# Gate and up products of eight feed-forward networks: one 512-column product for the high weights

## Chip, cores and metric

The kernel runs on one core of a Trainium2 chip. The metric is the device time of one execution in microseconds. Before the change the median of three runs is 2490.16 us (2488.91 to 2493.22).

## What is computed

Two transformer-like blocks of depth 2 work on 256 tokens of 1024 features in float32. Each layer of each block holds two feed-forward networks around a mixer, eight networks in all. What matters here is the network itself, in the first and in the second block:

```python
def swiglu(x, w_gate, w_up, w_down):
    return (jax.nn.silu(x @ w_gate) * (x @ w_up)) @ w_down
...
h = h + 0.5 * swiglu(rmsnorm(h, ffn1_norm[l]), ffn1_w_gate[l], ffn1_w_up[l], ffn1_w_down[l])
...
x = x + 0.5 * rms_norm(swiglu_2(rms_norm(x, ln_ffn1_pre[l]), w_ffn1_in[l], w_ffn1_out[l]),
                       ln_ffn1_post[l])
```

The weights are 1024 x 2816 (gate, up) and 2816 x 1024 (down). `swiglu_2` is the same with gate and up in one matrix. The second block's networks have a norm after them (the post norm) with an eps of its own.

## The kernel before

Activations lie feature-major: tiles of 128 features by 256 tokens. TensorE multiplies in the type float32r. So that float32 precision is kept, every operand is split into a high part (a copy rounded to float32r, on ScalarE, line 408) and a low part (the difference, on VectorE, line 409), in `split`. A product is the sum of three: high·high, high weights·low activations, low weights·high activations. `mm3` (line 325) issues these three for one k-tile of 128 features and 128 output columns, the weights stationary, 256 token columns moving.

`weights` (line 291) loads a weight chunk of 128 x 2048 in two halves of 512 KB (tag `raw`, four buffers, all on SP's queue in program order) and splits it in four parts of 512 columns (tags `wh` and `wl`, eight buffers each, hence two chunks). A part of a gate or up chunk holds two k-tiles of 256 output columns.

`gemm` (line 339) multiplies one chunk, or several together, over eight k-tiles: the k-tile is the outer loop, the two halves of 128 output columns the inner one. Both halves lie in one PSUM bank of 512 columns, 256 each. `ffn` (line 628) walks over 11 groups of 256 hidden features (`NG`). The first step runs gate 0, up 0 and gate 1 together; after that each step has a gate chunk, an up chunk and the down product of the step before. The gate result is multiplied by the token factor of the norm (line 662) and goes through silu (line 663), the up result is multiplied in (line 666), and the outcome is split into `hh` and `hl` for the down product, which sums in four banks (`acc`) over all steps. The last down product takes its weights from buffers of its own (`dh`, `dl`) and is issued in a chained order, each output tile being evacuated as it is done.

PSUM has eight banks: `mm` two, `st` one (norm sums), and in a feed-forward network `acc` four and `up` one. Gate uses `mm`, up uses `up` (in step 1 one of `acc`). `Act` holds the split activations as two separate sets of tiles (high, low), four feature tiles to an allocation.

`Norm.finish` (line 481) and `rstd` (line 370) give the token factor of a norm; it is applied after the product. `Post.finish` (line 584) computes the post norm of a second-block network: line 595 scales the sum of squares and adds eps, line 596 takes the power on GpSimd. The order of the instructions on each engine is found by the framework's scheduler, which simulates the program; only what is chained (`chain`) or loaded (`fetch`) keeps its written order.

Of the kernel before, what the change touches and what calls it, by code (L numbers as in the profile page):

```python
# [18 lines left out]
P = 128  # L19
# [192 lines left out]
# ---------------------------------------------------------------- device  # L212
# [8 lines left out]
def bc(x, n):  # L221
    """[128, m] repeated n times along a new middle dimension."""
    return x.unsqueeze(1).to_broadcast([x.shape[0], n, x.shape[1]])


class Net:
    def __init__(s, tc, ctx, A):
# [4 lines left out]
            dict(x=1, vec=1, cst=1, msk=1, mhalf=1, zero=1, cs=2, raw=4, wh=8, wl=8, act=8, sq=3, rb=3,  # L232
# [19 lines left out]
    # ---- allocation: a tag's tiles come in program order, each tag has its own buffers  # L252
# [58 lines left out]
    def chain(s, ins):  # L311
        """Issue behind the last chained instruction of its engine."""
# [12 lines left out]
    def mm3(s, out, w, c, n, a, start, stop, pin=lambda i: i):  # L325
        """Feature-major product of a k-tile: weight columns c..c+n stationary, a = (hi, lo) [128, 256]."""
        w = w.cols(c, n)
        for i, (x, y) in enumerate(((0, 0), (0, 1), (1, 0))):
            pin(s.nc.tensor.matmul(out, lhsT=w[x], rhs=a[y], start=start and i == 0,  # L329
                                   stop=stop and i == 2, skip_group_check=True))  # L330

    def mm3t(s, out, w, c, n, a, h, start, stop):
        """Token-major product of a k-tile, token half h: activations stationary."""
        w = w.cols(c, n)
        for i, (x, y) in enumerate(((0, 0), (1, 0), (0, 1))):
            s.nc.tensor.matmul(out, lhsT=a[y][:, h * P:h * P + P], rhs=w[x], start=start and i == 0,
                               stop=stop and i == 2, skip_group_check=True)
# [22 lines left out]
    def gemm_t(s, ap, act, tag="mm"):  # L360
        """Token-major: 256 output columns, both token halves in one bank."""
# [15 lines left out]
    def colsum(s, sq):  # L377
        """Sum over partitions of [128, 256] -> PSUM [128 tokens, 2]."""
# [6 lines left out]
    def spread_ps(s, r, pin=lambda i: i):  # L385
        """Per-token [128, 2] -> PSUM [128, 256] on every partition."""
# [6 lines left out]
    def warm(s, tag, n):  # L393
        """Products of zeros while TensorE waits: its clock halves after 3.4 us of rest."""
# [9 lines left out]
    def split(s, hi, lo, src, gain=None, pin=lambda i: i):  # L404
        """hi + lo = src * gain, each exact in float32r."""
# [9 lines left out]
class Weight:  # L415
    """A split weight chunk in parts of m columns."""
# [10 lines left out]
class Wide:  # L427
    """n feature tiles of [128, 256], four to an allocation, allocated at their first use."""
# [16 lines left out]
class Act:  # L445
    """Feature tiles split for the tensor engine."""

    def __init__(a, s, n, tag="act"):
        a.hi, a.lo = Wide(s, n, tag, F32R), Wide(s, n, tag, F32R)

    def __getitem__(a, k):
        return a.hi[k], a.lo[k]


class Norm:
    """RMS norm ahead of a GEMM: x * gain split as it is made, the token factor kept apart."""
# [6 lines left out]
    def tile(n, k, pin=lambda i: i):  # L463
        if n.gain:
            n.s.split(*n.act[k], n.s.x[:, k], n.s.v(n.gain, k), pin)
# [22 lines left out]
class Final(Norm):  # L488
    """The first block's final norm and the second's first: both token factors are left for after the GEMM."""
# [7 lines left out]
    def tile(n, k, pin=lambda i: i):  # L497
        n.s.split(*n.act[k], n.s.x[:, k], n.both[:, k:k + 1], pin)
# [11 lines left out]
    def finish(n):  # L510
# [8 lines left out]
        r2, _ = s.rstd(w, 2, D)  # L519
        nc.vector.tensor_tensor(n.r, n.r1, r2, op=ALU.mult)  # L520

# [7 lines left out]
class Post:  # L529
    """RMS norm of a GEMM's result (four banks of two tiles), added to the residual. The tiles come in ORDER:  # L530
    the last one alone is left when the rest have been summed."""
# [22 lines left out]
    def step(p, o, bank, late=False):  # L554
        """Tile o is in its bank [128, 2, 256]; `late` leaves the gain to scale()."""
# [14 lines left out]
        # all but the last three tiles in one  # L570
# [13 lines left out]
    def finish(p, eps, half, nxt, out=None):  # L584
        """eps: a number; half: a power of two"""
# [9 lines left out]
        s.chain(nc.vector.tensor_scalar(v, p.sum[:, 0:2], 1.0 / (D * half * half), eps / (half * half), op0=ALU.mult, op1=ALU.add))  # L595
# [32 lines left out]
def ffn(s, nrm, wg, wu, wd, evac, ws=None, ahead=None, pre=None, mid=None):  # L628
# [5 lines left out]
    def down(j, h, last):  # L634
# [6 lines left out]
        for kk, o in order:  # L641
            s.mm3(acc[o // 2][:, (o % 2) * T:(o % 2 + 1) * T], w, kk * D + o * P, P,
                  (h[0][:, kk], h[1][:, kk]), j == 0 and kk == 0 and o % 2 == 0, last and kk == 1,
# [4 lines left out]
    g2 = None  # L648
    for j in range(NG):
        if j == 0:  # L650
            g, u, g2 = s.gemm([wg[j], wu[j], wg[1]], act, ("mm", "up", "mm"), ws=ws)
# [26 lines left out]
FFN_SB = dict(ga=3, hh=3, hl=3, dh=4, dl=4)  # L678
# [3 lines left out]
def ffn_a(s, nrm, l, f, nxt, ws=None, ahead=None, pre=None, mid=None):  # L682
    """h += 0.5 * swiglu(rmsnorm(h))"""
# [77 lines left out]
def softmax_rows(s, sc):  # L761
    """sc [128, 2, nk] in SBUF -> exp(sc - max) in place, and 1/sum [128, 2]."""
# [9 lines left out]
def transposed(s, blocks):  # L772
    """Up to four [128, 128] blocks -> their transposes side by side in SBUF."""
# [18 lines left out]
def mix_a(s, nrm, l, nxt, ws, ahead):  # L792
    with s.phase("ma", dict(th=6, y=4, qk=4, cc=4, sc=3, pT=2, qm=2, lam=3, o8=2, **SMX),
# [4 lines left out]
def _mix_a(s, nrm, l, nxt, ws, ahead):  # L798
# [4 lines left out]
    # latents, pool input  # L803
# [8 lines left out]
    cqa = (s.t2("pT", F32R), s.t2("pT", F32R))  # L812
    for k in range(2):
        s.split(cqa[0][:, k], cqa[1][:, k], cq[:, k], s.v(f"a_qn_{l}", k))
    cka = (s.tile([P, T], "row", F32R), s.tile([P, T], "row", F32R))
    s.split(cka[0], cka[1], ckv, s.v(f"a_kvn_{l}"))
# [15 lines left out]
    # MLA up projections  # L832
# [3 lines left out]
    for c in range(3):  # L836
        b = s.ps("S")
        for k in range(2):
            for j in range(2):
                o = (2 * c + j) * P  # L840
                s.mm3(b[:, j * T:(j + 1) * T], wq, k * 768 + o, P, (cqa[0][:, k], cqa[1][:, k]), k == 0 and j == 0, k == 1)
# [39 lines left out]
    ym, yd, yp = Act(s, 4, "y"), Act(s, 4, "qk"), Act(s, 4, "y")  # L881
# [4 lines left out]
    pq = Act(s, 4, "th")  # L886
# [835 lines left out]
```

## Time and profile before

| | |
|---|---|
| median of three runs | 2490.16 us |
| lowest, highest run | 2488.91, 2493.22 us |
| profiled execution: span from first to last instruction | 2484.6 us |
| TensorE products | 19980 |
| TensorE, VectorE, ScalarE busy | 98%, 69%, 56% |
| mean granted clock of TensorE | 0.994 |

The profile is of one execution. Its page gives the span; what lies around the span in that execution is in no view, and the median of the runs is 5.56 us above it. PE is TensorE, PEld its weight loads, DVE VectorE, ACT ScalarE, POOL GpSimd and SP the queue that issues the loads. L329 is line 329 of the kernel; products of many places carry this line, so they are told apart by their tiles: `mm<-act,wh` writes a bank of the tag mm from activations and high weights. A matmul record lasts longer than the distance to the next one, because products are pipelined: the pace is read from starts or from a run of many.

### The profile page before, as it was taken

To read this page: it belongs to the slowest core of one execution; us is meant where nothing else is said; L and a number is where in the kernel's file an instruction comes from. 1 tells how busy PE (TensorE), PEld (TensorE's weight loads), DVE (VectorE), ACT (ScalarE), POOL (GpSimd) and SP (SyncE) were. 2 spreads that over 40 slices of the span, in tenths; PEclk is the share of its full clock that TensorE was granted. 3 is DMA by queue.
4 is the path that set the end of the run, shared out by engine and by line. 5 is a ranking of instruction groups with operands and counts; after the bars stand their busy time and mean duration, and the time that the engine had idled before them with its cause. 6 is when DMAs were issued, how large, how long until landed. Compare 5 with 4: busy or idle time off the path is not lost. (4 is left out here: it accounts for less than half of the span.)

```text
span 2484.6 us, 50434 instructions
## 1 busy us (share of the span) xinstructions
PE 2434.8 (98%) x19980; PEld 2390.1 (96%) x19980; DVE 1724.5 (69%) x3259; ACT 1381.2 (56%) x2598; POOL 42.9 (2%) x43
## 2 busy tenths in 40 slices
PE   8999999999999999999999999999999999999998
PEld 8999999999999989999999988999989998899997
DVE  6557888656756888865675588776666568877665
ACT  5556665555555676555555564465565556346554
POOL 0000000000000000000000000000000000000000
PEclk9999999999999999999999999999999999999999
DMA  6554444555555444555555532156535553215651
GB/s 228 184 186 156 144 140 170 192 185 191 173 184 184 142 147 145 170 195 182 176 182 183 189 129 85 37 171 205 187 111 179 186 197 120 85 43 170 205 191 59
DMA packets 110525, 396.91 MB, mean 160 GB/s; under 512 B 12752, under 2 KB 13264, under 8 KB 110288
## 3 DMA queue, kind: packets, MB, share of 16 engines
q1 hardware_dynamic: 109008, 391.33, 48.2%
q8 instruction: 156, 2.56, 0.4%
q10 hardware_dynamic: 1280, 2.36, 0.3%
q14 instruction: 81, 0.66, 0.1%
HBM read 392.60 MB, written 1.05 MB: 158 GB/s over the span
## 5 line engine op out<-in xcount | busy, mean ns | idle before, releaser
L409 DVE TENSOR_TENSOR wl<-raw,wh 128x512 fp32r<-128x512 f32 (+1 forms) x1446 | 984.0, 688 | 583.3 <-ACT wh L408 571.1
L408 ACT ACTIVATE wh<-raw 128x512 fp32r<-128x512 f32 (+1 forms) x1446 | 897.7, 628 | 842.8 <-PE mm L329 310.2
L329 PE MATMUL mm<-act,wh 128*128 128x256 f32 x4992 | 941.1, 286 | 18.6 <-ACT wh L408 9.0
L329 PEld LDWEIGHTS mm<-act,wh 128*128 128x128 f32 x4992 | 784.2, 191 | 27.9 <-ACT wh L408 9.3
L329 PE MATMUL mm<-act,wl 128*128 128x256 f32 x2496 | 709.3, 285 | 0.0
L329 PEld LDWEIGHTS mm<-act,wl 128*128 128x128 f32 x2496 | 476.8, 191 | 2.6 <-issue 1.7
L329 PE MATMUL up<-act,wh 128*128 128x256 f32 x2560 | 469.9, 284 | 0.8 <-ACT wh L408 0.8
L329 PEld LDWEIGHTS up<-act,wh 128*128 128x128 f32 x2560 | 401.6, 193 | 1.1 <-ACT wh L408 1.1
L329 PE MATMUL up<-act,wl 128*128 128x256 f32 x1280 | 363.2, 284 | 0.0
L329 PE MATMUL acc<-hl,wh 128*128 128x256 f32 x1280 | 358.6, 281 | 0.0
L329 PE MATMUL acc<-hh,wl 128*128 128x256 f32 x1280 | 358.6, 281 | 0.0
L329 PE MATMUL acc<-hh,wh 128*128 128x256 f32 x1280 | 357.5, 281 | 0.0
L329 PEld LDWEIGHTS up<-act,wl 128*128 128x128 f32 x1280 | 246.3, 192 | 0.0
L329 PEld LDWEIGHTS acc<-hh,wl 128*128 128x128 f32 x1280 | 243.1, 190 | 0.0
L329 PEld LDWEIGHTS acc<-hl,wh 128*128 128x128 f32 x1280 | 242.8, 190 | 0.0
L329 PEld LDWEIGHTS acc<-hh,wh 128*128 128x128 f32 x1280 | 242.0, 190 | 0.0
L666 DVE TENSOR_TENSOR ga<-up,ga 128x512 f32<-128x512 f32 x80 | 55.3, 691 | 18.3 <-PE up L329 13.3
L408 ACT ACTIVATE hh<-ga 128x512 fp32r<-128x512 f32 x88 | 55.5, 631 | 19.9 <-DVE ga L666 19.7
L662 DVE TENSOR_TENSOR ga<-mm,rb 128x512 f32<-128x512 f32 x88 | 60.0, 689 | 9.3 <-PE mm L329 9.3
L409 DVE TENSOR_TENSOR hl<-ga,hh 128x512 fp32r<-128x512 f32 x88 | 60.8, 691 | 6.1
L411 ACT ACTIVATE act<-x,vec 128x256 fp32r<-128x256 f32 x104 | 47.6, 500 | 28.1 <-DVE x L606 21.7
L663 ACT ACTIVATE ga<-ga 128x512 f32<-128x512 f32 x88 | 54.7, 629 | 14.6 <-DVE ga L662 14.5
(498 smaller groups left out, 2811.9 us busy)
## 6 DMA issues: line engine op xcount, KB each, us to landing
raw<-a_wgate SPq DMA_DIRECT2D x88, 512.0 KB, 3.7
raw<-a_wup SPq DMA_DIRECT2D x88, 512.0 KB, 3.8
raw<-a_wdown SPq DMA_DIRECT2D x88, 512.0 KB, 3.7
raw<-b_wgate SPq DMA_DIRECT2D x88, 512.0 KB, 4.0
raw<-b_wup SPq DMA_DIRECT2D x88, 512.0 KB, 4.1
raw<-b_wdown SPq DMA_DIRECT2D x88, 512.0 KB, 4.1
raw<-a_win SPq DMA_DIRECT2D x80, 512.0 KB, 3.7
raw<-a_wbr SPq DMA_DIRECT2D x24, 512.0 KB, 3.8
```

The costliest lines, as they stand in the source:

```text
L329: pin(s.nc.tensor.matmul(out, lhsT=w[x], rhs=a[y], start=start and i == 0, stop=stop and i == 2, skip_group_check=True))
L408: pin(nc.scalar.activation(hi, src, AF.Copy))
L409: pin(nc.vector.tensor_tensor(lo, src, hi.bitcast(F32), op=ALU.subtract))
L411: pin(nc.scalar.activation(hi, src, AF.Copy if isinstance(gain, float) else AF.Identity, scale=gain))
L662: nc.vector.tensor_tensor(ga, two(g), bc(rb, 2), op=ALU.mult)
L663: nc.scalar.activation(ga, ga, AF.Silu)
L666: nc.vector.tensor_tensor(ga, two(u), ga, op=ALU.mult)
```

## The change

For gate and up a new `mm2` takes the place of `mm3`: the high weights are loaded once and meet high and low activations in one product of 512 columns, which fills a bank (high·high in the first 256 columns, high·low in the second); the low weights meet the high activations in 256 columns, added to the first half. Each half of 128 output columns now has a bank of its own. A new `join` adds the two halves of each bank: ScalarE copies the second half to SBUF, VectorE adds the first. The loop over the halves is outermost for a chunk alone and innermost for the three chunks together. The banks of the later chunks are dealt in turn from `mm`, `mm`, `up`; the first three chunks use `mm` and all of `acc`.

So that high and low lie side by side, `Act` holds them in one tile; the mixers' uses of `Act` follow, with some temporary tiles under other tags, and the differential attention's result is split in two parts instead of one. The split of the network's hidden features goes into one tile `h`. The product with the token factor and the product with the gate read joined tiles in SBUF.

In second-block networks the eps of the post norm is multiplied by the token variance of the norm before it (`er`, one operation of 128x2 for a network), and line 595's operation takes `er` as an operand; `Final` multiplies its two variances.

```diff
+    def mm2(s, bank, w, c, a, start, stop):
+        hi, lo = w.cols(c, P)
+        s.nc.tensor.matmul(bank, lhsT=hi, rhs=a.rearrange("p a t -> p (a t)"), start=start, stop=False, skip_group_check=True)
+        s.nc.tensor.matmul(bank[:, :T], lhsT=lo, rhs=a[:, 0], start=False, stop=stop, skip_group_check=True)
+
+    def join(s, out, banks):
+        for i, b in enumerate(banks):
+            t = s.tile([P, T], "jn")
+            s.nc.scalar.activation(t, b[:, T:], AF.Copy)
+            s.nc.vector.tensor_tensor(out[:, i], b[:, :T], t, op=ALU.add)
+
+    def gemm2(s, aps, act, tags, ws=None):
+        ws = ws or s.weights(aps)
+        bs = [[s.ps(t) for t in tags[2 * i:2 * i + 2]] for i in range(len(ws))]
+        def tile(k, w, b):
+            for j in range(2):
+                s.mm2(b[j], w, k * T + j * P, act[k], k == 0, k == 7)
+        if len(ws) > 1:
+            for k in range(6):
+                for w, b in zip(ws, bs):
+                    tile(k, w, b)
+            for w, b in zip(ws, bs):
+                tile(6, w, b)
+                tile(7, w, b)
+        else:
+            for j in range(2):
+                for k in range(8):
+                    s.mm2(bs[0][j], ws[0], k * T + j * P, act[k], k == 0, k == 7)
+        return bs
...
+    order = ("mm", "mm", "up")
+    turn = [0]
+    def tags():
+        t = [order[(turn[0] + i) % 3] for i in range(2)]
+        turn[0] += 2
+        return t
...
-            g, u, g2 = s.gemm([wg[j], wu[j], wg[1]], act, ("mm", "up", "mm"), ws=ws)
+            g, u, g2 = s.gemm2([wg[j], wu[j], wg[1]], act, ("mm", "mm", "acc", "acc", "acc", "acc"), ws=ws)
+            turn[0] = 2
...
-            g, = s.gemm([wg[j]], act)
+            g, = s.gemm2([wg[j]], act, tags())
         ga = s.t2("ga")
-        nc.vector.tensor_tensor(ga, two(g), bc(rb, 2), op=ALU.mult)
+        s.join(ga, g)
+        nc.vector.tensor_tensor(ga, ga, bc(rb, 2), op=ALU.mult)
         nc.scalar.activation(ga, ga, AF.Silu)
         if j:
-            u, = s.gemm([wu[j]], act, ("acc" if j == 1 else "up",))
-        nc.vector.tensor_tensor(ga, two(u), ga, op=ALU.mult)
-        h = (s.t2("hh", F32R), s.t2("hl", F32R))
-        s.split(h[0], h[1], ga)
+            u, = s.gemm2([wu[j]], act, tags())
+        uu = s.t2("uu")
+        s.join(uu, u)
+        nc.vector.tensor_tensor(ga, uu, ga, op=ALU.mult)
+        h = s.tile([P, 2, 2, T], "h", F32R)
+        s.split(h[:, :, 0], h[:, :, 1], ga)
...
-FFN_SB = dict(ga=3, hh=3, hl=3, dh=4, dl=4)
+FFN_SB = dict(ga=3, uu=2, jn=4, h=3, dh=4, dl=4)
...
+    er = s.tile([P, 2], "er")
+    s.nc.vector.tensor_scalar(er, nrm.var, 4 * EPS, None, op0=ALU.mult)
...
-    post.finish(EPS, 0.5, nxt)
+    post.finish(er, 0.5, nxt)
...
-        s.chain(nc.vector.tensor_scalar(v, p.sum[:, 0:2], 1.0 / (D * half * half), eps / (half * half), op0=ALU.mult, op1=ALU.add))
+        if isinstance(eps, float):
+            s.chain(nc.vector.tensor_scalar(v, p.sum[:, 0:2], 1.0 / (D * half * half), eps / (half * half), op0=ALU.mult, op1=ALU.add))
+        else:
+            s.chain(nc.vector.scalar_tensor_tensor(v, p.sum[:, 0:2], 1.0 / (D * half * half), eps, op0=ALU.mult, op1=ALU.add))
...
-                    s.split(yd.hi.quad(0)[:, :, ts], yd.lo.quad(0)[:, :, ts], four(tb), nlam[:, 1:2])
+                    for i in range(2):
+                        hi, lo = yd.pair(i)
+                        s.split(hi[:, :, ts], lo[:, :, ts], four(tb)[:, 2 * i:2 * i + 2], nlam[:, 1:2])
```

## Rows read from the trace of the kernel before

**Rows 1.** The page's first part: busy us of each engine (share) xinstructions
```profile
PE 2434.8 (98%) x19980; PEld 2390.1 (96%) x19980; DVE 1724.5 (69%) x3259; ACT 1381.2 (56%) x2598; POOL 42.9 (2%) x43
```

**Rows 2.** Chain of waits, last feed-forward network: start us, us, what
```profile
2278.88 5.76 PE up L329 x48
2284.64 5.76 PE acc L329 x48
2290.40 5.76 PE mm L329 x48
```

**Rows 3.** The page's costliest groups: count | busy, mean ns | idle before, releaser
```profile
L409 DVE TENSOR_TENSOR wl<-raw,wh 128x512 fp32r<-128x512 f32 (+1 forms) x1446 | 984.0, 688 | 583.3 <-ACT wh L408 571.1
L408 ACT ACTIVATE wh<-raw 128x512 fp32r<-128x512 f32 (+1 forms) x1446 | 897.7, 628 | 842.8 <-PE mm L329 310.2
L329 PE MATMUL mm<-act,wh 128*128 128x256 f32 x4992 | 941.1, 286 | 18.6 <-ACT wh L408 9.0
...
L329 PE MATMUL mm<-act,wl 128*128 128x256 f32 x2496 | 709.3, 285 | 0.0
```

**Rows 4.** TensorE's timeline around 512-column products: start us, us, engine, what
```profile
244.18 0.40 PE L336 MATMUL S<-wh,row 128*128 128x512 f32 x1
244.41 0.40 PE L336 MATMUL S<-wl,row 128*128 128x512 f32 x1
244.65 0.39 PE L336 MATMUL S<-wh,row 128*128 128x512 f32 x1
244.88 0.28 PE L329 MATMUL mm<-act,wl 128*128 128x256 f32 x1
244.99 0.40 PE L329 MATMUL mm<-act,wh 128*128 128x256 f32 x2
```

**Rows 5.** Plain float32 products (timeline, record min/median/max ns), and a faster down stretch
```profile
299.65 1.89 PE L984 MATMUL S<-cc,qm 128*128 128x256 f32 x8
...
L1204 PE MATMUL rw<-rp,ra x32: 377/378/382, 1505.7 to 2144.9; 128*128 128x256 f32 x32
...
460.18 0.28 PE L329 MATMUL acc<-hl,wh 128*128 128x256 f32 x1
...
461.20 0.28 PE L329 MATMUL acc<-hh,wl 128*128 128x256 f32 x1
```

**Rows 6.** Groups by line, shapes apart, of ScalarE and VectorE
```profile
L401 ACT ACTIVATE rb<-st 128x256 f32<-128x256 f32 x21 | 8.0, 382 | 11.6 <-PE st L389 11.5
...
L663 ACT ACT_TABLE_LOAD x5 | 6.4, 1283 | 0.1
...
L662 DVE TENSOR_TENSOR ga<-mm,rb 128x512 f32<-128x512 f32 x88 | 60.0, 689 | 9.3 <-PE mm L329 9.3
L666 DVE TENSOR_TENSOR ga<-up,ga 128x512 f32<-128x512 f32 x80 | 55.3, 691 | 18.3 <-PE up L329 13.3 <-ACT ga L663 5.0
...
L603 DVE TENSOR_TENSOR yg<-yg,st 128x256 f32<-128x256 f32 x16 | 6.0, 418 | 19.4 <-PE st L389 19.4
```

**Rows 7.** Busy us of each engine in a steady stretch, granted clock, DMA
```profile
2285.00:2405.00 120.00, 120.00 (x1002) 120.00 (x1002) 72.59 (x110) 63.20 (x103) 0.00 (x0) 1.00 0.60 194
```

**Rows 8.** ScalarE's timeline in the same network
```profile
2309.08 0.63 ACT L408 ACTIVATE wh<-raw 128x512 fp32r<-128x512 f32 x1 [0.80 <-PE mm L329]
```

**Rows 9.** SP's timeline there, and the page's load issues (last number: us to landing)
```profile
2311.92 3.20 SPq L289 DMA_DIRECT2D raw<-b_wup  x2
...
raw<-b_wup SPq DMA_DIRECT2D x88, 512.0 KB, 4.1
```

**Rows 10.** Chain of waits at the start and end of that network
```profile
2267.36 2.52 PE mm L329 x21
...
2271.44 5.28 PE acc L329 x44
...
2422.88 5.88 PE acc L329 x49
```

**Rows 11.** Line 595: duration ns min/median/max
```profile
L595 DVE TENSOR_SCALAR v<-st x8: 159/159/160, 1433.5 to 2473.8; 128x2 f32<-128x2 f32 x8
```

More of the change, by code (lines that the diff above doesn't have):

```diff
@@ L328, in mm3 @@
         for i, (x, y) in enumerate(((0, 0), (0, 1), (1, 0))):
-            pin(s.nc.tensor.matmul(out, lhsT=w[x], rhs=a[y], start=start and i == 0,
+            pin(s.nc.tensor.matmul(out, lhsT=w[x], rhs=a[:, y], start=start and i == 0,
                                    stop=stop and i == 2, skip_group_check=True))
+    def mm2(s, bank, w, c, a, start, stop):
[25 more added lines that the diff above has]
+        return bs
     def mm3t(s, out, w, c, n, a, h, start, stop):
@@ L335, in mm3t @@
         for i, (x, y) in enumerate(((0, 0), (1, 0), (0, 1))):
-            s.nc.tensor.matmul(out, lhsT=a[y][:, h * P:h * P + P], rhs=w[x], start=start and i == 0,
+            s.nc.tensor.matmul(out, lhsT=a[:, y, h * P:h * P + P], rhs=w[x], start=start and i == 0,
                                stop=stop and i == 2, skip_group_check=True)
@@ L445, with __init__, group, halves @@
 class Act:
-    def __init__(a, s, n, tag="act"):
-        a.hi, a.lo = Wide(s, n, tag, F32R), Wide(s, n, tag, F32R)
-    def __getitem__(a, k):
-        return a.hi[k], a.lo[k]
+    def __init__(a, s, n, tag="act", per=4):
+        a.s, a.tag, a.per, a.ts = s, tag, per, {}
+    def group(a, i):
+        if i not in a.ts:
+            a.ts[i] = a.s.tile([P, a.per, 2, T], a.tag, F32R)
+        return a.ts[i]
+    def __getitem__(a, k):
+        return a.group(k // a.per)[:, k % a.per]
+    def halves(a, k, n):
+        t, o = a.group(k // a.per), k % a.per
+        return t[:, o:o + n, 0], t[:, o:o + n, 1]
+    def pair(a, b):
+        return a.halves(2 * b, 2)
 class Norm:
@@ L464, in tile @@
         if n.gain:
-            n.s.split(*n.act[k], n.s.x[:, k], n.s.v(n.gain, k), pin)
+            a = n.act[k]
+            n.s.split(a[:, 0], a[:, 1], n.s.x[:, k], n.s.v(n.gain, k), pin)
     def squares(n, b):
@@ L497, in tile @@
     def tile(n, k, pin=lambda i: i):
-        n.s.split(*n.act[k], n.s.x[:, k], n.both[:, k:k + 1], pin)
+        a = n.act[k]
+        n.s.split(a[:, 0], a[:, 1], n.s.x[:, k], n.both[:, k:k + 1], pin)
     def squares(n, b):
@@ L642, in down @@
             s.mm3(acc[o // 2][:, (o % 2) * T:(o % 2 + 1) * T], w, kk * D + o * P, P,
-                  (h[0][:, kk], h[1][:, kk]), j == 0 and kk == 0 and o % 2 == 0, last and kk == 1,
+                  h[:, kk], j == 0 and kk == 0 and o % 2 == 0, last and kk == 1,
                   s.chain if last else lambda i: i)
@@ L792, in mix_a @@
 def mix_a(s, nrm, l, nxt, ws, ahead):
-    with s.phase("ma", dict(th=6, y=4, qk=4, cc=4, sc=3, pT=2, qm=2, lam=3, o8=2, **SMX),
+    with s.phase("ma", dict(th=6, y=2, qk=4, cc=4, sc=3, pT=2, qm=2, lam=3, o8=2, **SMX),
                  dict(S=2, PT=2, O=1)):
@@ L811, in _mix_a @@
     nc.vector.tensor_tensor(kr, bk[:32, T:], rb[:32], op=ALU.mult)
-    cqa = (s.t2("pT", F32R), s.t2("pT", F32R))
+    cqa = s.tile([P, 2, 2, T], "th", F32R)
     for k in range(2):
-        s.split(cqa[0][:, k], cqa[1][:, k], cq[:, k], s.v(f"a_qn_{l}", k))
-    cka = (s.tile([P, T], "row", F32R), s.tile([P, T], "row", F32R))
-    s.split(cka[0], cka[1], ckv, s.v(f"a_kvn_{l}"))
+        s.split(cqa[:, k, 0], cqa[:, k, 1], cq[:, k], s.v(f"a_qn_{l}", k))
+    cka = s.t2("qm", F32R)
+    s.split(cka[:, 0], cka[:, 1], ckv, s.v(f"a_kvn_{l}"))
     sq = s.t2("sc")
@@ L896, in _mix_a @@
         nc.vector.tensor_tensor(m[:, :16], m[:, :16], pin[:, st, :16], op=ALU.subtract)
-        s.split(*pq[st], m)
+        s.split(pq[st][:, 0], pq[st][:, 1], m)
         cur = dst
@@ L908, in _mix_a @@
                                     op0=ALU.add, op1=ALU.mult)
-            s.split(*yp[g], y)
+            s.split(yp[g][:, 0], yp[g][:, 1], y)
     dqk = Wide(s, 8, "cc")
@@ L957, in mla @@
                 ts = slice(qt * P, (qt + 1) * P)
-                s.split(ym.hi.quad(0)[:, :, ts], ym.lo.quad(0)[:, :, ts], four(ob))
+                hi, lo = ym.halves(0, 4)
+                s.split(hi[:, :, ts], lo[:, :, ts], four(ob))
             yield
@@ L1048, in _mix_a @@
                 if n == 1:
-                    s.split(ma.hi.pair(2 * hf + i), ma.lo.pair(2 * hf + i), m, 0.5)
+                    s.split(*ma.pair(2 * hf + i), m, 0.5)
     def add(b, ps):
@@ L1547, in mix_b @@
         y = Act(s, 8)
-        rw = rwkv(s, nrm, l, rb, first, wrk, y.hi.pair(3), y.lo.pair(3))
+        rw = rwkv(s, nrm, l, rb, first, wrk, *y.pair(3))
         next(rw)
         with s.phase("mb1", dict(att=2, va=1, cm=1, so=1, nu=1, sink=1, km=1, vt=1, sc=3, pT=1), dict(S=1, PT=1, O=1)):
-            ml = mlstm(s, nrm, l, rb, wif, y.hi.pair(2), y.lo.pair(2))
-            sw = swa(s, nrm, l, rb, y.hi.quad(0), y.lo.quad(0))
+            ml = mlstm(s, nrm, l, rb, wif, *y.pair(2))
+            sw = swa(s, nrm, l, rb, *y.halves(0, 4))
             def items():
@@ L1615, in block_b @@
         m = Norm(s, f"b_mxi_{l}")
-        with s.phase("fb", dict(yg=4, **FFN_SB), FFN_PS):
+        with s.phase("fb", dict(yg=4, er=1, **FFN_SB), FFN_PS):
             ws = ffn_b(s, n, l, 1, m, ws, ahead_b(s, l), tables if l == 0 else None)
@@ L1635, in early @@
                 s.fetch(pt, A["pT"][l])
-                pa.extend((s.t2("pt", F32R), s.t2("pt", F32R)))
-                s.split(pa[0], pa[1], pt)
+                pa.append(s.tile([P, 2, 2, T], "pt", F32R))
+                s.split(pa[0][:, :, 0], pa[0][:, :, 1], pt)
                 pw.extend(s.weights([A["b_wpp"][l]], tags=("ph", "pl")))
```

15 lines of the change are left out of this document (8 added, 7 removed).

## The prediction

> **What bounds the kernel now.** I began with the busy shares of the engines: TensorE is busy for 98% of the span, VectorE for 69%, ScalarE for 56% [rows 1]. The reader is to see that only TensorE can be the bound over most of the run. A share proves nothing for one stage, so next came the chain of waits in a feed-forward stage: it consists of TensorE alone, up, acc, mm, up, acc, each 48 products in 5.76 us [rows 2], which is 120 ns a product with no gap between. There the time falls only if TensorE gets through the same sums faster, or rises if something makes it wait. The costliest groups are the fixed work around it: splitting weights takes 688 ns on VectorE and 628 ns on ScalarE for each 512 columns, and the products of a weight's high part are twice as many as those of its low part (4992 against 2496) [rows 3]: each high part is loaded and used twice.
>
> **What the change does to TensorE.** A k-tile of a gate or up product was three products of 256 columns (high·high, high·low, low·high). It becomes one of 512 and one of 256. The columns stay the same, 768; what goes is one product and one weight load. There are 8 feed-forward networks of 22 gate or up chunks, each chunk with 8 k-tiles of 2 halves: 8 x 22 x 16 = 2816 such pairs. Before, each takes 3 x 120 = 360 ns [rows 2].
>
> So everything hangs on what a 512-column product costs. The trace has a few, with a split weight as the moving operand. Three follow each other at 244.18, 244.41 and 244.65, the next 256-column product starts at 244.88 and the one after at 244.99 [rows 4]: 0.70 us for three, or 233 ns each, and 0.34 us for the last of them with its follower. A 512-column product therefore costs nearly twice 120, not 120 plus the bare columns: a large saving is not there. By the mean, a pair is 233 + 120 = 353 ns. By the one place where 512 is followed by 256, as in the new stream, it is 340 ns. I take 350, nearer to the mean, because long runs of 256 settle at 120 whatever came before. That saves 10 ns a pair, 2816 x 10 = **28.2 us**.
>
> The bounds: no gain if 512 columns settle at 2 x 120 in long runs (360). On the other side, plain float32 products of 256 columns, which pass each column twice, run eight in 1.89 us; one record lasts 378 ns, so seven spacings fill the other 1.51 us, 216 ns each. And one stretch of the down product runs at 113 ns instead of 120 (460.18 to 461.20 for nine) [rows 5]. That is 216 + 113 = 329 ns, a gain of 31 ns a pair or 87 us. A loss on TensorE itself I exclude: no columns are added, and a load is dropped.
>
> A rule speaks here for less. The Trainium skill, "TensorE: Matmul & The Clock Gate", section "Back-to-back issue gap", has a stream at its columns over 2.4 GHz plus about 2.5 ns. By it a dropped product would save an estimated 2.5 ns and the whole change 7 us. The 120 ns of [rows 2] are not the 109 that it would give for 256 columns.
>
> **What is added beside TensorE.** A gate or up chunk now fills two banks, each joined by a ScalarE copy out of PSUM and a VectorE addition, 128x256 both. The nearest rows are 382 ns for a copy from PSUM and 418 ns for a VectorE operation with a PSUM operand [rows 6]. There are 352 joins: 352 x 0.382 = 134 us on ScalarE, 352 x 0.418 = 147 us on VectorE. The product with the gate stays one 512-wide operation each (L662 and L666, 689 and 691 ns [rows 6]). In the steady stretch VectorE is busy 72.6 and ScalarE 63.2 of 120 us [rows 7]; with four joins per 17.28 us (about 28 per 120 us) they reach 84 and 74. Both stay below TensorE, so the cost is **0** as long as no join holds a bank back; if TensorE were not the cover, it would be 0.8 us a join.
>
> The cover has to hold at three places. **Weights:** ScalarE splits a part as soon as TensorE lets its buffer go, with idle time of 0.80 us before [rows 8]; there are eight buffers, two chunks ahead. A single chunk now goes through all k-tiles for its first half, then again for its second, so its four parts come free only in the second half (2.8 us) instead of over 5.76. They are wanted two chunks later: 11.2 less 3.5 leaves 7.7 us, against four splits of 0.69, 2.8 us. Behind a split that waits for TensorE stand the joins in ScalarE's queue, see the third rival. **Loads:** count and order on SP's queue stay; a load lands in 4.1 us and two are issued for each chunk [rows 9]; with raw buffers for two chunks they have 5.6 us and more. **Banks:** gate and up take two of three banks in turn, so the second bank of an up product is the first of the gate product before it. From its last product to its reuse lie two half chunks, 2 x 2.8 = 5.6 us; a join needs 0.38 + 0.42 = 0.8.
>
> **The ends of a network.** At the start three chunks run together and the two of acc must be joined before the first down product. That product starts at 2271.44, and TensorE already fills the time before it with gate products of chunk 2 [rows 10]. Six joins add 6 x 0.42 = 2.5 us to VectorE there, near an activation-table load of 1.28 us [rows 6]. Bounds 0 and 8 x 1 us; I take **+1 us** in all. At the tail, the last up product is followed by the down product of the chunk before, 49 products in 5.88 us, before its result is wanted [rows 10]; the new path behind it is 0.38 + 0.42 + 0.69 + 0.63 + 0.69 = 2.8 us, covered, **0**.
>
> **The small edits.** The eps correction adds a VectorE operation on 128x2 in each of four networks, one in the norm between the blocks, and turns four of L595 into another form; L595 takes 159 ns [rows 11]. Nothing but two-element rows is computed; under 1 us together, **0**. The mixers get other buffers for the same bytes, and four split pairs more (the differential attention's result in two parts); beside TensorE, **0**, bounds -3 and +3 us, as the order of instructions may shift.
>
> **Sum:** 2484.6 - 28.2 + 1 = 2457.4 us of span. The page gives no more than the span; the median of the runs, 2490.16, stands 5.6 us above it. Forecast **2463 us**.
>
> **Rivals.**
> 1. *The weight loads set the pace of 256-column products.* Then 512 columns hide a load and run at their bare 216 ns. For it: plain float32 products, whose loads come half as often, show no more than their bare 216 [rows 5]. Against it: three 512-column products with loads as sparse took 233 each [rows 4]. A pair would be 216 + 120 = 336, 24 ns saved, 67.6 us: 2491.2 - 67.6 = 2424 us. Chance 0.10. The Trainium skill, same page, section "LDWEIGHTS (loading the stationary operand)", puts a load at its columns over 1.2 GHz, an estimated 107 ns here, just the time of 256 columns; by it this rival holds, and [rows 4] speak against it.
> 2. *The change saves nothing:* 512 columns settle at 240 ns. For it: 233 is 97% of that, and plain columns are then the only price. Time 2490.2 + 1 = 2491 us. Chance 0.13. The rule of the Trainium skill on the gap belongs here: with its estimated 7 us the same case ends at 2484.
> 3. *A bank comes late (the slower side).* In ScalarE's queue a join's copy stands behind splits that wait for TensorE to free weights in the second half of the same chunk, 2.8 us after the bank is full; with a split (0.63) and the join (0.8) that is 4.2 of the 5.6 us. It decides once another 1.4 us of work (two more splits, or the gate's activation and its wait) is put ahead. If each of the 80 later up products then waits 0.5 us, 40 us come back: 2463 + 40 = 2503 us. For it: idle times on ScalarE end with TensorE throughout [rows 8]. Against: VectorE and ScalarE keep a quarter and more of their time. Chance 0.14, with ends from 2490.
>
> **How the numbers follow.** The forecast has 0.63 and its own range, pairs of 345 to 356 ns, is 2447 to 2480 us. About 0.2% (5 us) is what a measurement of this kernel can tell from no change. Faster by more: forecast and rival 1, 0.73. Within: rival 2, 0.13. Slower: rival 3, 0.14. The range takes in rival 2, the nearer ends of rival 3 and the gains up to 20 ns a pair (56 us): 2436 to 2495.
>
> **What would show it.** In the chain of the changed kernel a gate or up chunk takes 5.60 us instead of 5.76, a down product 5.76 as before; products fall by 2816 to 17164. 512-column products follow at 230 ns and 256-column ones at 120. Idle time of TensorE stays below 20 us in the FFN groups; if it shows waits for the join's addition (on VectorE), rival 3 is right; a chunk of 5.38 us speaks for rival 1, one of 5.76 for rival 2. The forecast is wrong if the pace of the down products changes too, for which no row gives a reason.

## The result, and the profile after

| | before | after |
|---|---|---|
| median of the runs timed together (four each) | 2489.97 us | 2462.89 us |
| lowest, highest | 2488.91, 2493.22 | 2461.86, 2469.30 |
| profiled execution: time, span | not shown, 2484.6 | 2463.42, 2461.6 us |

The ratio is 0.9899 (95%: 0.9883 to 0.9915): 27 us faster, as forecast. The profiled execution after stands 1.8 us above its span, and so does every other execution of which both are known: by that measure the execution profiled before was a quick one of its kernel. Span against span the gain is 23.0 us.

The page after, the engines and the costliest groups (the columns of [rows 1] and [rows 3]):

```profile
PE 2400.8 (98%) x17164; PEld 2232.8 (91%) x17164; DVE 1854.3 (75%) x3620; ACT 1476.0 (60%) x2954; POOL 43.6 (2%) x43
...
L336 PE MATMUL mm<-act,wh 128*128 128x512 f32 x1728 | 614.0, 395 | 13.0 <-ACT wh L444 8.9 <-DVE act L448 4.1
L337 PE MATMUL mm<-act,wl 128*128 128x256 f32 x1728 | 482.8, 280 | 0.7 <-DVE wl L445 0.7
...
L343 ACT ACTIVATE jn<-mm 128x256 f32<-128x256 f32 x216 | 80.1, 371 | 83.7 <-PE mm L337 83.6
...
L344 DVE TENSOR_TENSOR ga<-mm,jn 128x256 f32<-128x256 f32 x112 | 46.9, 419 | 64.7 <-ACT jn L343 64.7
```

TensorE made 2816 products fewer. The joins cost what was taken for them (371 and 419 ns), and the costly gate and up groups hardly wait: 8.9 of their 13.0 us is the start of the program, 9.0 before.

The chain of waits in the last network, to be read beside [rows 2]:

```profile
2282.56 5.65 PE acc L329 x48
...
2299.31 5.65 PE acc L329 x48
```

From one down product to the next pass 16.75 us, 17.28 before. The 48 products of the down take 5.65 instead of 5.76; 16.75 - 5.65 = 11.10 us remain for gate and up, 32 pairs of **347 ns**. TensorE's timeline in another network of the second block, to be read beside [rows 4]:

```profile
1723.99 0.39 PE L336 MATMUL mm<-act,wh 128*128 128x512 f32 x1
1724.22 0.28 PE L337 MATMUL mm<-act,wl 128*128 128x256 f32 x1
1724.34 0.40 PE L336 MATMUL mm<-act,wh 128*128 128x512 f32 x1
...
1725.73 0.39 PE L336 MATMUL mm<-act,wh 128*128 128x512 f32 x1
```

Five pairs in 1.74 us. Over whole networks the starts give 230.3 + 116.6 ns in the second block, 232.1 + 115.1 in the first, 236 + 117 (353) in the first network alone.

The sum over the starts of all products in the two traces (distance beyond 25 ns over the usual one is put down as waiting, of the product that the gap follows): gate and up -32.8 us by pace, +2.5 by waiting; down -4.2 by pace, **+9.9 by waiting**; everything else +0.9. That is -23.7. (Counted for the product that the gap precedes, the down products wait 11.6 us more instead of 9.9.) Two of these terms were not forecast: the down products' pace and their waiting. Both were followed up.

The waiting stands ahead of the last down product of a network, as TensorE's waits tell (total us, times, longest):

```profile
PE acc L329 <- ACT h L444: 5.0, 6, 1.9
...
PE acc L329 <- DVE h L445: 1.9, 6, 0.3
```

and ScalarE's and TensorE's timelines at the end of the first network of the second block tell why:

```profile
1407.19 1.15 ACT L444 ACTIVATE wh<-raw 128x512 fp32r<-128x512 f32 x2 [1.19 <-DMA raw<-b_win_r]
1408.25 0.36 ACT L343 ACTIVATE jn<-mm 128x256 f32<-128x256 f32 x1
1408.51 1.14 ACT L444 ACTIVATE wh<-raw 128x512 fp32r<-128x512 f32 x2
1410.71 0.63 ACT L444 ACTIVATE h<-ga 128x512 fp32r<-128x512 f32 x1 [1.06 <-DVE ga L733]
...
1411.40 0.52 PE L329 MATMUL acc<-h,dh 128*128 128x256 f32 x1 [1.85 <-ACT h L444]
1412.12 0.58 PE L329 MATMUL acc<-h,dh 128*128 128x256 f32 x1 [0.21 <-DVE h L445]
```

The copy for the network's last join (1408.25) stands in ScalarE's queue behind splits of the *next* stage's weights, one of which waited 1.19 us for its load. Addition, product, split `h` and the last down product follow late. And TensorE then runs slower for a while; windows before, in and after that stretch (the column after POOL is the granted clock):

```profile
1405.00:1409.00 4.00, 4.00 (x36) 4.00 (x35) 1.84 (x3) 2.44 (x5) 0.00 (x0) 1.00 0.38 153
1411.40:1414.50 3.10, 2.89 (x12) 2.60 (x13) 1.70 (x3) 1.55 (x4) 0.00 (x0) 0.52 0.65 201
1415.00:1419.00 4.00, 4.00 (x36) 4.00 (x35) 1.70 (x4) 2.38 (x5) 0.00 (x0) 1.00 0.00 1
```

The granted clock falls from 1.00 (2.4 GHz) to 0.52 (1.2 GHz) after the idle time, so that this end cost 3.9 us: its 48 last products took 9.68 us instead of 5.76. Five other networks lost 1.2 to 1.75 us in the same way, at a granted clock of 1.00. In the sixth and the last network TensorE did not wait for `h`.

### The profile page after: what moved, and what is told of

It reads as the page before. It is cut to its first block, busy times and chain, and to the rows that moved or that the text cites. A ratio compares the mean times of both kernels' runs of the same rounds, so it can differ in the third digit from the quotient of the medians.

```text
span 2461.6 us, 45601 instructions
## 1 busy us (share of the span) xinstructions
PE 2400.8 (98%) x17164; PEld 2232.8 (91%) x17164; DVE 1854.3 (75%) x3620; ACT 1476.0 (60%) x2954; POOL 43.6 (2%) x43
## 5 line engine op out<-in xcount | busy, mean ns | idle before, releaser
L336 PE MATMUL mm<-act,wh 128*128 128x512 f32 x1728 | 614.0, 395 | 13.0 <-ACT wh L444 8.9
L329 PE MATMUL acc<-h,wh 128*128 128x256 f32 x2560 | 457.0, 280 | 0.0
L329 PE MATMUL mm<-act,wh 128*128 128x256 f32 (+1 forms) x2176 | 420.7, 289 | 9.5 <-ACT act L447 3.4
L336 PEld LDWEIGHTS mm<-act,wh 128*128 128x128 f32 x1728 | 324.5, 188 | 85.4 <-ACT wh L444 9.1
L329 PEld LDWEIGHTS acc<-h,wh 128*128 128x128 f32 x2560 | 391.2, 188 | 4.0 <-ACT h L444 0.3
L329 PEld LDWEIGHTS mm<-act,wh 128*128 128x128 f32 (+1 forms) x2176 | 341.5, 190 | 15.8 <-ACT act L447 4.5
L329 PE MATMUL acc<-h,wl 128*128 128x256 f32 x1280 | 355.7, 279 | 0.0
L336 PE MATMUL up<-act,wh 128*128 128x512 f32 x832 | 296.4, 394 | 0.1
L329 PEld LDWEIGHTS acc<-h,wl 128*128 128x128 f32 x1280 | 240.5, 188 | 0.3
L336 PEld LDWEIGHTS up<-act,wh 128*128 128x128 f32 x832 | 156.3, 188 | 34.3 <-DVE uu L344 0.5
```

The costliest lines, as they stand in the source:

```text
L329: pin(s.nc.tensor.matmul(out, lhsT=w[x], rhs=a[:, y], start=start and i == 0, stop=stop and i == 2, skip_group_check=True))
L336: s.nc.tensor.matmul(bank, lhsT=hi, rhs=a.rearrange("p a t -> p (a t)"), start=start, stop=False, skip_group_check=True)
```

## The experiments

Twelve kernels, each an edit of the changed one unless said otherwise. Times are medians of the runs, ratios are to the kernel before run beside them.

**1. Three products again, the rest of the change kept**

```diff
-        s.nc.tensor.matmul(bank, lhsT=hi, rhs=a.rearrange("p a t -> p (a t)"), ...)
+        s.nc.tensor.matmul(bank[:, :T], lhsT=hi, rhs=a[:, 0], ...)
+        s.nc.tensor.matmul(bank[:, T:], lhsT=hi, rhs=a[:, 1], ...)
```

> The changed kernel with the 512-column product taken apart into two products of 256 (same banks, same loop order, same joins; high weights loaded twice again). Theory A (the gain is the pace of the 512-column product with its 256-column follower: 347 ns in the changed kernel's trace against 360): gate and up go back to 120 ns a product, 2816 x 13 = 36 us come back, 2495 to 2503 us, and the waits at the ends of the networks stay. Rival B (the gain is from the new order, banks and buffers): stays within 5 us of 2463.

Measured: 2489.82 us, ratio 0.9993 (0.9984 to 1.0002). Chain of waits:

```profile
2305.66 5.66 PE acc L329 x48
2322.84 5.66 PE acc L329 x48
```

17.18 - 5.66 = 11.52 us for 96 products: 120 ns again. The pace is theory A's, the time lies below its range: by the starts, gate and up gave some 33 us back and TensorE waited 6 us less in all. With the buffers where they lie here, all of the gain, 27 us, hangs on the 512-column product; joins, banks and layout together gain nothing, as the quicker down products and the waits at the ends of the networks about cancel. The down product stays at 5.66, so its quicker pace is not the work of the 512-column stream.

**2. The splits for the next stage held behind the last `h`.** On each engine the splits that prefetch for the next stage are ordered behind that engine's part of the last split of hidden features.

```diff
+            s.hold = dict(marks)
             ready.append(ahead and ahead())
+            s.hold = {}
...
-        s.split(h[:, :, 0], h[:, :, 1], ga)
+        s.split(h[:, :, 0], h[:, :, 1], ga, pin=mark)
```

> The changed kernel with the next stage's weight splits (the last loads of a network) ordered behind the split of the last hidden features on ScalarE and VectorE. Theory A (the last join's copy stands in ScalarE's queue behind splits that wait for loads of the next stage, and so the last down product waits 1 to 4 us in a network): the idle time before the products of the last down product goes from about 10 us to under 2 us, 2451 to 2456 us. Rival (the longer path of copy, addition and products is itself too long, or the splits are then missing at the start of the next stage): no gain, 2461 us or more.

Measured: 2454.28 us, ratio 0.9853 (0.9840 to 0.9867), 8.6 us below the changed kernel. The last down products, from the groups of each kernel, the changed one first, then this one:

```profile
L329 PE MATMUL acc<-h,dh 128*128 128x256 f32 x256 | 50.3, 293 | 7.1 <-ACT h L444 5.0 <-DVE h L445 1.9
```

```profile
L333 PE MATMUL acc<-h,dh 128*128 128x256 f32 x256 | 46.4, 283 | 0.0
```

The 7.1 us of idle time are gone, the mean product is back from 293 to 283 ns as no stretch at the lower clock is left among them, and the 48 last products take 5.76 us in each network. The mechanism is shown, as theory A had it, and this is the fastest version.

**3. Loads of the high and low weights paired.** For a chunk alone two k-tiles go together: 512, 512, 256, 256.

```diff
-                for k in range(8):
-                    s.mm2(bs[0][j], ws[0], k * T + j * P, act[k], k == 0, k == 7)
+                for k in range(0, 8, 2):
...
+                    for i, (w, a) in enumerate(p):
+                        s.nc.tensor.matmul(b, lhsT=w[0], rhs=a.rearrange("p a t -> p (a t)"), start=k + i == 0, stop=False, skip_group_check=True)
+                    for i, (w, a) in enumerate(p):
+                        s.nc.tensor.matmul(b[:, :T], lhsT=w[1], rhs=a[:, 0], start=False, stop=k + i == 7, skip_group_check=True)
```

> The changed kernel with two k-tiles taken together in chunks computed alone: two 512-column products, then two of 256. Theory A1 (a 512-column product is dearer before another 512 than before a 256, 236 against 230, and a 256 before a 256 costs 120 against 117): a pair costs 351, 2432 pairs, about 11 us more, 2474 us. Rival A2 (the price goes with columns and loads, whatever follows): within 3 us of 2463.

Measured: 2462.23 us (0.9886, 0.9871 to 0.9902), the changed kernel's time, as rival A2 said. Timeline:

```profile
1723.30 0.62 PE L368 MATMUL mm<-act,wh 128*128 128x512 f32 x2
1723.77 0.40 PE L370 MATMUL mm<-act,wl 128*128 128x256 f32 x2
1724.00 0.63 PE L368 MATMUL mm<-act,wh 128*128 128x512 f32 x2
```

Four products in 0.70 us: 349 ns a pair, 233.0 + 115.9 by all starts, 2 ns above the changed kernel's second block and 2 below A1's price; in the second block the down products beside it run at 116.7 ns instead of 117.6. Neighbours of the same width hardly change the price, so the columns carry nearly all of it: 2 x 116.6 - 230.3 is 2.9 ns in the changed kernel's second block, 2 x 115.1 - 232.1 is -1.9 ns in its first. What a second product costs beyond its columns is no larger than these shifts and cannot be read from them.

**4. No joins.** The later steps read the first half of a bank only; the product high·low is computed and left out of the sum.

```diff
-        s.join(ga, g)
-        nc.vector.tensor_tensor(ga, ga, bc(rb, 2), op=ALU.mult)
+        for i in range(2):
+            nc.vector.tensor_tensor(ga[:, i], g[i][:, :T], rb, op=ALU.mult)
```

> The changed kernel without the joins: the products of high weights with low activations are computed and left out of the sum; the first halves are read straight from PSUM, in two operations of 256 columns each. Theory A (joins cost nothing except at the ends of networks, where the last copy waits behind other splits): the waits at the ends go, 2450 to 2456 us. Rival (joins also delay the banks within the networks or at their start): below 2448 us. Rival (the waits at the ends have another cause): 2461 us or more.

Measured: 2471.87 us (0.9924, 0.9911 to 0.9936), 9 us **slower** than with the joins. By the number that is the last rival's range, by its reason it is not, and no theory had a loss: the tail wait shrinks from 12.0 to 3.0 us, as the queue is shorter, but a new wait stands in TensorE's list:

```profile
PE mm L336 <- DVE ga L727: 3.9, 4, 1.2
```

Without the join the first reader of a gate bank is the product with the norm's token factor, so the bank stays held until the factor is there. The join empties it earlier: its 0.8 us buy freedom at the start of a network. By the starts of the products, each gap counted for the product behind it, gate and up products wait 11.3 us more than in the changed kernel and products outside the networks 3.7 us more. The wait for the banks is 3.9 us of it. TensorE's granted clock shows another part: 0.988 to 0.990 in the five runs, 0.991 to 0.993 in the changed kernel's four, and in the profiled executions the products inside the stretches at the lower clock lost some 5 us more than in the changed kernel. Why the clock falls more often here is not settled.

**5. The halves innermost for single chunks too**

```diff
-            for j in range(2):
-                for k in range(8):
-                    s.mm2(bs[0][j], ws[0], k * T + j * P, act[k], k == 0, k == 7)
+            for k in range(8):
+                tile(k, ws[0], bs[0])
```

> The changed kernel with the two halves of 128 output columns innermost for a single chunk too, so that both banks of a chunk fill together and a weight part is let go after a quarter of the chunk, as before the change. If rival 3 of the prediction (banks held by joins behind splits) bears on the steady stretch in either order, this shows TensorE waits for the joins: both banks end together and two joins follow at once, the first bank wanted again after 2.8 us instead of 5.6. Theory: a join is done 0.8 to 1.6 us after its bank, so no wait in the steady stretch, pairs at 347 ns as before, stall at the ends of networks changed by some us at most: 2458 to 2468 us. Rival: 0.5 us lost for each of 160 chunks: 2500 us or more.

Measured: 2470.07 us (0.9918, 0.9904 to 0.9932): outside the theory's range, far from the rival's. TensorE waits for a join's addition twice, 0.3 us each; the pair itself is slower, 235.5 + 117.0 = 352.5 ns in the second block, 349.7 in the first. So the order of the halves moves the pace of TensorE without a wait to match, and the third rival of the prediction has no place in the steady stretch in either order.

**6. Only layout, single `h` and eps correction kept; gate and up as before, no joins**

```diff
-            g, = s.gemm2([wg[j]], act, tags())
+            g, = s.gemm([wg[j]], act)
...
-            u, = s.gemm2([wu[j]], act, tags())
+            u, = s.gemm([wu[j]], act, ("acc" if j == 1 else "up",))
```

> Only the new activation layout, the single tile h and the eps correction are kept; gate and up are the old three 256-column products into one bank, without joins. Theory L (the new layout of the activations and of h is what quickens the down products of the second block): down products there follow at 117.8 ns, gate and up 256s at 120.0, gain of 4 us over the kernel before: 2484 to 2487 us, and the stall ahead of the last down products is below 3 us. Rival G (the quicker down products come from the changed gate and up stream next to them, through buffers or weight loads): down products at 120.0 in the second block, 2489 to 2491 us.

Measured: 2482.52 us (0.9971, 0.9960 to 0.9983). Chain of waits:

```profile
2295.01 5.76 PE up L329 x48
2300.77 5.66 PE acc L329 x48
2306.43 5.75 PE mm L329 x48
```

Gate and up at 120, down at 118: theory L's picture, 7.6 us in all, somewhat more than its range had. What of these three edits does it was left to the next two.

**7. Hidden features in two tiles again**

```diff
-        h = s.tile([P, 2, 2, T], "h", F32R)
-        s.split(h[:, :, 0], h[:, :, 1], ga)
+        h = (s.t2("hh", F32R), s.t2("hl", F32R))
+        s.split(h[0], h[1], ga)
```

> The changed kernel with the hidden features in two tiles again, high and low. Theory L1 (the single tile h, high and low side by side, is what quickens the down products of the second block): they follow at 120.0 ns again, 4 us lost: 2466 to 2468 us. Rival L2 (it is not h; the down pace hangs on something else of the change): 117.8 ns, 2461 to 2465 us.

Measured: 2463.60 us (0.9898, 0.9882 to 0.9913), a down product still 5.65 us, L2's range. L1 fell: it is not `h`.

**8. The eps correction undone** (a different eps in the post norms)

```diff
-        nc.vector.tensor_tensor(n.var, n.var, v2, op=ALU.mult)
...
-    er = s.tile([P, 2], "er")
-    s.nc.vector.tensor_scalar(er, nrm.var, 4 * EPS, None, op0=ALU.mult)
...
-    post.finish(er, 0.5, nxt)
+    post.finish(EPS, 0.5, nxt)
```

> The changed kernel with the eps correction undone (the post norms get the plain eps again, the final norm does not multiply its variances). Theory: some twenty operations on two columns beside 98% busy TensorE are worth nothing: 2461 to 2465 us. Rival: the order of instructions shifts around the norms and moves the stall ahead of the last down products: off by 2 to 8 us either way, read there and not at line 595.

Measured: 2471.38 us (0.9928, 0.9916 to 0.9941). Five operations on two columns, four of them of 160 ns each in the changed kernel, and 8.5 us. The theory fell, and the rival has about the size but not the place; the chain shows where:

```profile
2293.34 5.75 PE acc L329 x48
2310.40 5.75 PE acc L329 x48
```

The down product is back at 120 ns, and (17.06 - 5.75) / 32 = 353 ns is the pair. The whole second block runs at another pace; the first block, which has no `er`, is as it was. What the edit leaves out beside the operations is an 8-byte tile at the head of the second block's buffers. The program's buffers are laid one behind the other in units of 32 bytes (no view of the profile shows that, the next experiment tests it), so without `er` all of that block's own buffers, `h` first of all, lie 32 bytes lower. The weights and the activations, in an earlier pool, stay where they are.

**9. Correction undone, the tile kept:** `er` is filled with zeros and read by nothing (eps as in 8).

```diff
+    er = s.tile([P, 2], "er")
+    s.nc.vector.memset(er, 0.0)
```

> The eps correction stays undone, but the 8-byte tile er stands again at the head of the second block's buffers (filled with zeros once a network, read by nothing), so that the hidden features and everything behind it lie 32 bytes further on, as in the changed kernel. Theory P (the 8.5 us that undoing the correction cost is a matter of where the buffers lie, h relative to the weights above all): second block back at down products of 117.8 ns and pairs of 347, 2461 to 2465 us. Rival O (the operation, its order or its values set the pace): 120.0 and 353 as without the correction, 2469 to 2473 us.

Measured: 2463.86 us (0.9900, 0.9885 to 0.9915).

```profile
2284.27 5.65 PE acc L329 x48
2301.02 5.65 PE acc L329 x48
```

16.75 and 5.65, the changed kernel to the hundredth. It is the place of the buffers, not the operation: theory P.

**10. The kernel before, with 32 unused bytes** behind the activations

```diff
         raws = []
+        if s.pad is None:
+            s.pad = s.tile([P, 8], "pad")
+            s.nc.vector.memset(s.pad, 0.0)
```

> The kernel before with nothing but 32 unused bytes put between the activations and all buffers behind them (weights, hidden features). Counted modulo 128 bytes, the activations stay at 32, the weights move from 32 to 64, the hidden features from 96 (first block) and 32 (second block) to 0 and 64. Theory R (what counts is how the moving operand lies against the weights; equal offsets give 120 ns, others 118): gate and up, 32 against 32 until now, fall from 120 to 118, 8448 x 2 = 17 us less, and the second block's down products, now 64 against 64, stay at 120: 2470 to 2475 us. Theory H (the offset of the moving operand alone decides, 32 is slow): gate and up stay at 120, the second block's down products fall to 118: 2484 to 2488 us. Rival N: no change, 2488 to 2493 us.

Measured: 2470.88 us, ratio 0.9926 (0.9914 to 0.9939): 18.5 us below the kernel before, with none of the change. Chain of waits, beside [rows 2]:

```profile
2282.61 5.68 PE up L333 x48
2288.29 5.75 PE acc L333 x48
2294.04 5.68 PE mm L333 x48
```

Gate and up fall from 120.0 to 118.3 ns in all eight networks; the second block's down products, now on equal offsets with their weights, stay at 119.7. Theory R has it, time and pace: for products of 256 columns equal offsets of moving operand and weights are the slow case, at 32 as at 64. H and N fell. A check that needs no new run: the last down product of each network takes weights from `dh` and `dl`, which lie in the same pool as the hidden features and only buffers of whole multiples of 128 bytes further on, so its offsets are always equal. It runs at 119 to 120 ns in every network of every run, also where the other down products run at 117 to 118.

**11. Experiment 2 with the 32 bytes of experiment 10**

> The changed kernel with the pinned splits of the tail experiment and the same 32 unused bytes behind the activations. Modulo 128 bytes: activations 32, weights 64, hidden features 0 (first block) and 96 (second block), so nothing meets its equal. Theory S (equal offsets also cost the changed stream): the pair falls from 347 ns to 340 to 344, the 353 ns of the first network go, 2435 to 2447 us. Rival T (the pair of 512 and 256 is at its floor at 347; what equal offsets cost was in the three short products alone, and so was most of what the change gained): only the first network gains, 2450 to 2455 us. Beside the padded kernel before (2470.9) and its own tail gain of 8.6 us, T leaves the change itself 8 to 12 us, S 15 to 27.

Measured: 2457.41 us (0.9867, 0.9853 to 0.9882), 3 us **more** than without the bytes. Both theories miss. Pairs: 233.9 + 118.6 = 352.5 ns in the first block, 231.9 + 117.9 = 349.8 in the second. The pair of 512 and 256 does not follow the rule of the three short products: its quick 347 ns came with activations and weights on equal offsets, and unequal ones do not better it. In the second block the steps alternate between 16.91 and 16.70 us from one down product to the next, with every buffer where it was.

**12. The same with 64 bytes**

```diff
-            s.pad = s.tile([P, 8], "pad")
+            s.pad = s.tile([P, 16], "pad")
```

> The same with 64 unused bytes: modulo 128, activations 32, weights 96, hidden features 32 (first block) and 0 (second block). Theory: any unequal offset does, so within 4 us of the version with 32 bytes. Rival: the distance of 64 bytes against 32 matters, off by 5 us or more, seen alike in all gate and up products, where the distance doubles.

Measured: 2454.63 us (0.9853, 0.9829 to 0.9877), within 4 us of the version with 32 as the theory said, but not by its reason: the pair is at 353 ns in both blocks, gate and up together 13 us more than in the changed kernel by pace, while the products outside the networks run some 13 us quicker by pace and wait some 6 us longer. This ties with experiment 2; it is no better.

## Why the prediction came out as it did

**What the change does to TensorE: right, 350 forecast, 347 measured** (353 in the first network). The argument of [rows 4], that a 512-column product costs nearly twice a 256-column one, held: 230 to 236 against 115 to 117. The term was 28.2 us and measured 32.8. Rival 1 (weight loads set the pace) has no support: with loads as sparse as the change makes them 512 columns still cost 230 and not 216, and pairing them (experiment 3) changes a pair by 2 ns. Its 216 ns, and those of the far bound, were measured for 512 columns of this type in no run. They come from 256 columns of plain float32; that these are passed twice is a reading of their time (216 ns, against 109 for 256 columns of bf16 zeros, line 397, in the trace before). Rival 2 (nothing saved) fell by experiment 1 beside the result.

But the price of the old stream was taken as given, and that was luck. 120 ns was the slow one of two paces, set by where the buffers lie. With no change at all, 32 unused bytes take 18.5 us off (experiment 10). Beside that kernel, at 2470.88, the changed one is 8.0 us quicker, and 16.6 with its splits held (experiment 2). Against three short products at 118.3 (355 ns) a pair of 350 to 353 saves 2 to 5 ns, 6 to 14 us over 2816 pairs. The Trainium skill, "TensorE: Matmul & The Clock Gate", section "Back-to-back issue gap", has the formula from which the prediction estimated 2.5 ns for a dropped product; the section calls it the gap of an isolated product. The 2 to 5 ns of the padded streams lie near that estimate, the 13 ns that change and before show side by side do not. The formula's own paces, 109 and 216 ns, were reached by no stream of this type here. The prediction set the rule against [rows 2] because 120 was not 109; a part of that difference, about 2 ns, was placement.

**The small edits: eps 0. Failed, as a step.** The operations do cost nothing (experiment 9 leaves them out: +1 us, within the measurement). The 32 bytes that their tile takes are worth 8.5 us: by the starts of the two profiles, whose spans lie further apart than the medians (2474.8 and 2461.6 us), 4.3 in the down products and about 7 in the pairs. Here belongs "the forecast is wrong if the pace of the down products changes too, for which no row gives a reason": it changed, 120.0 to 117.6. A sign of it did stand in [rows 5], taken as a bound only: down products at 113 ns in one block (118 over the whole block) while [rows 2] has 120 in the other, same line and shape.

**The ends of a network: tail "covered, 0". Failed, +9.9 us.** The path of 2.8 us behind the last up product was rightly sized and is shorter than the cover of 5.88. What was left out is the queue: the scheduler put splits of the next stage's weights ahead of the last join's copy, and one of them waited for a load. That is rival 3's mechanism, a join's copy behind splits, but at the network's end, not in each chunk. By its own price (0.5 us for each up product) it was wrong; experiment 2 gives 8.6 us for it. Waiting in gate and up grew by 2.5 us, where +1 was taken for the starts.

Two ends of the stated ranges are 1 to 2 us off the prediction's own sums: pairs of 345 ns give 2449 and not 2447 us, a gain of 20 ns a pair 2435 and not 2436. Nothing hangs on it.

**Joins beside TensorE: 0, right in the steady stretch.** With or without them the pair stays at 347 ns (experiment 4), and no wait for a join of any weight stands in TensorE's list. At the starts they even help.

So the forecast of 2463 stands on a right mechanism and on two errors of 8 to 10 us that cancel, which was luck. Without the shift by `er` the change would have given 2471; without the tail's wait, 2454.

## What to carry to other kernels

Before costing the removal of instructions, look whether the pace of the old stream is the same everywhere in the trace: equal shapes at 118 and 120 ns on one line can be a sign that placement sets a part of the price, and a few unused bytes between buffers are the cheaper experiment. When a step is added to an in-order queue, check at the end of each stage what prefetch for the next one the scheduler puts ahead of it, and pin it behind. After any edit that adds a buffer, however small, compare the pace of streams that the edit does not touch.

## What the runs showed of the hardware that was not expected

The offset between operands moves TensorE's pace at a granted clock of 1.00 and without any wait in the trace. Offsets are counted modulo 128 bytes, worked out from the sizes and the order in which the program lays its buffers; no view of the profile shows them.

| stream | moving operand / weights | ns a product |
|---|---|---|
| gate and up, 3 x 256 (before) | 32 / 32 | 120.0 |
| gate and up, 3 x 256 (experiment 10) | 32 / 64 | 118.3 |
| down, second block (before; experiment 8) | 32 / 32 | 120.0; 119.9 |
| down, second block (experiment 10) | 64 / 64 | 119.7 |
| down, second block (after) | 64 / 32 | 117.6 |
| down, second block (experiment 11) | 96 / 64 | 116.8 |
| down, first block (after) | 96 / 32 | 117.8 |
| last down of a network (every run) | equal | 119 to 120 |
| pair 512 + 256, second block (after; experiment 8) | 32 / 32 | 347; 353 |
| pair, second block (experiments 11; 12) | 32 / 64; 32 / 96 | 349.8; 353 |

Streams of 256-column products follow one rule here: equal offsets are slow. A distance of 64 bytes counts as unequal (117.8 at 96 / 32). The pair does not: in the changed kernel and in experiment 8 its own operands lie alike, and only the buffers of the down products and joins beside it moved, yet it runs at 347 in one and 353 in the other, the same in every step of a network; in experiment 11 the steps alternate. A stream seems to settle into one of a few rhythms that depends on what ran just before it. That is argued, not shown; which memory or queue makes it stays open, as no experiment moved the weights against each other or the bank alone.

A wait of 1.85 us ahead of a last down product was followed, in one of eight networks, by some 3 us at a granted clock of 0.52, which doubled its cost (3.9 us); after a wait of 0.88 us in another network it stayed at 1.00.
